# Transposing memory and seven token tiles by DMA instead of on TensorE in a two-layer decoder trunk

## The chip, the cores and the metric

The kernel runs on one core of one Trainium2 chip. The metric is the device time of one execution in microseconds (us). The kernel before takes 2338.09 us, the median of three runs (2337.59 to 2340.59).

## The reference, cut to what matters

The trunk has two layers. Each layer is a half-weighted SwiGLU block, a mixing block with three branches (stick-breaking attention, forgetting attention, attention to a memory), and a second half-weighted SwiGLU block, with an RMSNorm ahead of and behind each of them. There are 512 tokens of width 1024 and 256 memory rows of the same width, all float32.

```python
mem_n = _rmsnorm(mem, mem_norm_g)
for l in range(DEPTH):                                   # 2
    f = _swiglu(_rmsnorm(h, ffn1_pre_g[l]), ...)
    h = h + 0.5 * _rmsnorm(f, ffn1_post_g[l])

    u = _rmsnorm(h, mix_pre_g[l])
    proj = u @ w_in[l]
    ...
    k_mem, v_mem = jnp.split(mem_n @ w_mem_kv[l], 2, axis=-1)
    o_mem = _memory_attention(_split_heads(q_mem, ...), ...)
    ...
    h = h + _rmsnorm(merged @ w_out[l], mix_post_g[l])

    f = _swiglu(_rmsnorm(h, ffn2_pre_g[l]), ...)
    h = h + 0.5 * _rmsnorm(f, ffn2_post_g[l])
```

The normalised tokens `u` and the normalised memory `mem_n` are left factors of matrix products, so the kernel needs each of them with the features on the partitions: both must be transposed.

## The kernel before, in words

The 512 tokens are four tiles of 128 tokens by 1024 features (tile 0 to 3, `t`). To keep float32 accuracy on TensorE (PE), each operand is split into a high part `h` (a copy rounded by ScalarE, ACT) and a low part `l` (source minus high part, on VectorE, DVE); `mm3` issues three matmuls for each product, on source lines L212, L213 and L214. `split` makes the parts (L182 and L183, or L185 and L186 with a scale). So every weight block that arrives by DMA in a `raw_...` tile costs ACT a cast into `wh_...` of 128x1024 and DVE a subtraction into `wl_...`; only two `raw` buffers and four `wh` and four `wl` buffers exist for most of them, and SyncE (SP) issues all weight transfers from one queue in program order.

The place where one block ends and the next begins is called a border here. A class `Sub` handles it, with one object for each border: `a0` and `a1` stand between the first SwiGLU and mixing of layer 0 and layer 1, `b0` and `b1` between mixing and the second SwiGLU, `c0` between the two layers. At a border the last down projection (PSUM tiles `pda`, `pwo`, `pdc`) gives for each token tile:

- `result`: sums of squares (`sq...`, L544) and the scaled rows into a tile `fa`, `fb` or `fc`;
- `residual` (L575): the new token rows into `hfa`, `hm` or `hfc`, then their squares (L544 again);
- `normed` (L582): the normalised rows `u` back into `fa`, `fb`, `fc`, after a small chain of one-column steps (L486 to L500);
- `turned` (L592): eight PE transposes of 128x128 into two PSUM banks `uta`, `utb`, `utc`, and from there `split` with the scale into `us_a`, `us_b`, `us_c` (two ACT rows and two DVE rows of 128x512).

`chain` is the generator that does this for one tile, and `Q.weave` interleaves the chains with the queue of matrix products: a chain says ("wait", microseconds) for how much PE work is to be put in between. A scheduler then fixes one order of instructions for each engine when the program is built, and the engines run in that order, each waiting for what its next instruction needs.

At the borders `a0` and `a1` the memory is prepared too. `mem_norm` loads the two memory tiles `mraw` (128x1024), multiplies them by their reciprocal norms (L1063), transposes them with 16 PE transposes into PSUM tiles `mt` (L1070), and makes `mn` from these in eight ACT rows (L1075) and eight DVE rows (L1076) of 128x256, with the gain `memg`, which stands one feature to a partition. Then come the products for the memory's keys (`pmk`, weights `mk`) and values (`pmv`, weights `mv`), which need `mn` but no token; and then the first product that needs all four token tiles, the memory queries `pqm<-us_a,wh_qm`. Its job has the condition `src.ready(range(NT))`. At the borders `b` and `c` the first product (`pgc`, `pga`, L668) needs tiles 0 and 1.

Two 16-bit DMA transposes are already in the kernel before: in the token products (`turn`, L814, L815, L822, half planes of 128x1024 16-bit words) and in the stick-breaking heads (L1152, L1161, L1237).

The buffers that matter: the tag `rs` has one buffer of 128x1024 float32, and `v` has six.

Of the kernel before, what the change touches and what calls it, by code (L numbers as in the profile page):

```python
# [18 lines left out]
P = 128  # L19
# [4 lines left out]
def kernel(  # L24
# [57 lines left out]
    cst = ctx.enter_context(tc.tile_pool(name="cst", bufs=1))  # L82
# [6 lines left out]
    ident = cst.tile([P, P], F32, name="ident")  # L89
# [9 lines left out]
    def tmp(name):  # L99
        return sb.tile([P, S], F32, tag="f32t", bufs=8, name=name)  # L100
# [3 lines left out]
    def stile(shape, tag, name, dt=F32R):  # L104
        return sb.tile(shape, dt, tag=tag, bufs=BUFS[tag], name=name)
# [9 lines left out]
    memg = cst.tile([P, ND], F32, name="memg")  # L115
# [63 lines left out]
    def split(h_ap, l_ap, src, scale=None, later=False):  # L179

        if scale is None:
            both = [nc.scalar.copy(h_ap, src)]  # L182
            make = lambda: nc.vector.tensor_tensor(l_ap, src, h_ap.bitcast(F32), ALU.subtract)  # L183
# [173 lines left out]
    class Queue:  # L357
# [83 lines left out]
        def spawn(self, chain):  # L441
            self.chains.append([self.t, chain])
# [33 lines left out]
    HF = (slice(0, S), slice(S, D))  # L476
# [7 lines left out]
    RS = -16.0  # L484

    def rstd(st, a, b=None, beside=None):  # L486
# [13 lines left out]
        nc.vector.scalar_tensor_tensor(y, w, -3.0, y, ALU.add, ALU.mult)  # L500
        return y

    class Sub:

        def __init__(self, name, g_post, g_pre, half, tag, slack=0.0):

            self.slack = slack
# [93 lines left out]
    W_H, W_U = 4.8, (8.0, 7.0, 6.5, 4.5)  # L608


    NG = 2
# [5 lines left out]
    def ffn(l, src, wg, wu, wd, dst, name, spare, parked, plan, aside=None):  # L617
# [348 lines left out]
        if name == "a0":  # L966
            Q.add([], vectors)
# [69 lines left out]
    mem_rstd = cst.tile([P, MT, 2], F32, name="mem_rstd")  # L1037
# [10 lines left out]
    def mem_norm(l, mn):  # L1048

        mn[:] = [stile([P, ND, M], "tri", f"mn{l}_{i}") for i in range(2)]  # L1050
        raws = []
        if l == 0:
            ms, r = mem_rstd[:, :, 0], mem_rstd[:, :, 1]
            for out_, in_, f, s in ((r, ms, AF.Ln, 1.0), (r, r, AF.Exp, -0.5)):
                tc.keep_in_program_order(nc.scalar.activation(out_, in_, f, scale=s))
            nc.vector.tensor_tensor(ms, ms, r, ALU.mult)
            nc.vector.tensor_tensor(ms, ms, r, ALU.mult)
            nc.vector.tensor_scalar(ms, ms, -0.5, 1.5, ALU.mult, ALU.add)
            nc.vector.tensor_tensor(r, r, ms, ALU.mult)
        for t in range(MT):  # L1060
            raw = stile([P, D], "v", f"mraw{l}_{t}", F32)
            nc.sync.dma_start(raw[:], mem[0, t * P:(t + 1) * P, :])
            nc.vector.tensor_scalar(raw[:], raw[:], mem_rstd[:, t, 1:2], None, ALU.mult)  # L1063
            raws.append(raw)
        yield 0.0
        for i in range(ND // 2):
            pt = pbank("z", f"mt{l}_{i}")
            for j in range(2):
                for t in range(MT):
                    nc.tensor.transpose(pt[:, j * M + t * P:j * M + (t + 1) * P],  # L1070
                                        raws[t][:, (2 * i + j) * P:(2 * i + j + 1) * P], ident[:])
            for j in range(2):
                d = 2 * i + j
                src = pt[:, j * M:(j + 1) * M]
                nc.scalar.activation(mn[0][:, d], src, AF.Copy, scale=memg[:, d:d + 1])  # L1075
                nc.vector.scalar_tensor_tensor(mn[1][:, d], src, memg[:, d:d + 1],  # L1076
                                               mn[0][:, d].bitcast(F32), ALU.mult, ALU.subtract)
            yield 0.45

    def mem_kv(l, mn, ks, vs):  # L1080

# [539 lines left out]
    kvs = [([], []) for _ in LAYERS]  # L1621
    subs = [Sub("x", None, (0, 0), False, "k")]
    for l in LAYERS:
        subs.append(Sub(f"a{l}", (1, l), (2, l), True, "k", 4.0))
        subs.append(Sub(f"b{l}", (3, l), (4, l), False, "v"))
        subs.append(Sub(f"c{l}", (5, l), (0, l + 1) if l < L - 1 else None, True, "k"))

    def warm(n):

# [97 lines left out]
    for l in LAYERS:  # L1727
        i, mn = 3 * l, []
# [43 lines left out]
```

## Time and profile before

| | us |
|---|---|
| median of three runs | 2338.09 |
| lowest and highest run | 2337.59, 2340.59 |
| the profiled execution, its own time | 2342.67 |
| its span in the profile | 2340.9 |
| PE, PE's weight loads, DVE, ACT busy | 2322.9, 1960.2, 1764.2, 1509.8 |

The span runs from the first to the last recorded instruction; the profiled execution took 1.8 us more than its span and 4.6 us more than the median of the runs. A row of a timeline gives the start in us from the span's start, the length in us, the engine, the source line and what was written from what; in square brackets stands for how long the engine had been idle and what ended that. SPq is SyncE's queue of DMA issues.

### The profile page before, as it was taken

What the parts mean: (1) busy time and instruction counts of PE and PEld (TensorE: products, weight loads), DVE (VectorE), ACT (ScalarE), POOL (GpSimd) and SP (SyncE); (2) the same over time, 40 slices, a digit from 0 to 9 for tenths busy, and PEclk for the clock granted to TensorE, in tenths of its full rate; (3) what the DMA queues carried; (4) which work ended last, traced back from release to release, by engine and by line L of the source; (5) the groups of instructions that cost most, each with busy time, mean ns of one, the idle gap of its engine ahead of it and who ended that gap; (6) DMA issues with size and microseconds to landing.
All of it is one profiled execution on the core that took longest, in us unless ns stands there. A gap on an engine that the chain in (4) does not pass through costs nothing.

```text
span 2340.9 us, 30650 instructions
## 1 busy us (share of the span) xinstructions
PE 2322.9 (99%) x11463; PEld 1960.2 (84%) x11463; DVE 1764.2 (75%) x2253; ACT 1509.8 (64%) x2216; POOL 81.2 (3%) x182
## 2 busy tenths in 40 slices
PE   9999999999999999999999999999999999999998
PEld 7888888888888888888898888888888888888887
DVE  8877877566777688878798788765677767887785
ACT  6677465577756556775656774655787674667744
POOL 0000000000111000000000000000001100000000
PEclk9999999999999999999999999999999999999999
DMA  6667454344423555674646665544444236466744
GB/s 207 190 176 221 146 189 141 93 115 114 122 73 105 187 186 164 185 199 152 226 144 186 196 185 179 185 114 95 119 105 116 81 118 200 160 195 176 220 138 144
DMA packets 340344, 365.44 MB, mean 156 GB/s; under 512 B 120778, under 2 KB 231650, under 8 KB 340196
## 3 DMA queue, kind: packets, MB, share of 16 engines
q1 hardware_dynamic: 340100, 363.46, 52.0%
q8 instruction: 90, 1.47, 0.3%
q14 instruction: 58, 0.48, 0.1%
q0 software_dynamic: 96, 0.03, 0.0%
HBM read 319.39 MB, written 16.78 MB: 144 GB/s over the span
## 4 chain that ended last, share of the span: by engine, by line
PE 85%; DMA 5%; ACT 4%; DVE 3%; issue 2%; DVEq 0%; SPq 0%; ACTq 0%
PE pg L213 4%; PE pg L212 4%; PE pg L214 4%; PE pda L213 3%; PE pda L212 3%; PE pda L214 3%; PE pdc L213 3%; PE pdc L212 3%; PE pdc L214 3%; PE pb L213 1%; PE pb L212 1%; PE pb L214 1%; PE pq L213 1%; PE pq L212 1%; PE pq L214 1%
## 5 line engine op out<-in xcount | busy, mean ns | idle before, releaser
L212 PE MATMUL pg<-us_a,wh_wg 128*128 128x512 f32 x384 | 150.4, 392 | 0.0
L213 PE MATMUL pg<-us_a,wh_wg 128*128 128x512 f32 x384 | 149.7, 390 | 0.0
L214 PE MATMUL pg<-us_a,wl_wg 128*128 128x512 f32 x384 | 149.6, 390 | 0.0
L183 DVE TENSOR_TENSOR wl_da<-raw_da,wh_da 128x1024 fp32r<-128x1024 f32 x50 | 60.8, 1223 | 44.6 <-ACT wh_da L182 44.4
L183 DVE TENSOR_TENSOR wl_dc<-raw_dc,wh_dc 128x1024 fp32r<-128x1024 f32 x50 | 61.0, 1223 | 44.1 <-ACT wh_dc L182 44.1
L213 PE MATMUL pdc<-wl_dc,ahc 128*128 128x512 f32 x224 | 87.7, 392 | 0.0
L213 PE MATMUL pda<-wl_da,aha 128*128 128x512 f32 x224 | 87.6, 391 | 0.0
L214 PE MATMUL pdc<-wh_dc,alc 128*128 128x512 f32 x224 | 87.2, 389 | 0.0
L214 PE MATMUL pda<-wh_da,ala 128*128 128x512 f32 x224 | 87.2, 389 | 0.0
L212 PE MATMUL pdc<-wh_dc,ahc 128*128 128x512 f32 x224 | 86.6, 390 | 0.5 <-ACT pdc L895 0.5
L212 PE MATMUL pda<-wh_da,aha 128*128 128x512 f32 x224 | 86.5, 389 | 0.0
L186 DVE SCALAR_TENSOR_TENSOR wl_wg<-raw_wg,wh_wg 128x1024 fp32r<-128x1024 f32 x48 | 58.7, 1223 | 35.8 <-ACT wh_wg L185 35.6
L214 PEld LDWEIGHTS pg<-us_a,wl_wg 128*128 128x128 f32 x384 | 72.1, 188 | 15.1
L212 PEld LDWEIGHTS pg<-us_a,wh_wg 128*128 128x128 f32 x384 | 72.1, 188 | 14.2
L213 PEld LDWEIGHTS pg<-us_a,wh_wg 128*128 128x128 f32 x384 | 72.1, 188 | 14.2
L182 ACT CAST wh_da<-raw_da 128x1024 fp32r<-128x1024 f32 x50 | 52.1, 1050 | 46.9 <-PE pda L214 19.4
L182 ACT CAST wh_dc<-raw_dc 128x1024 fp32r<-128x1024 f32 x50 | 52.3, 1049 | 46.0 <-DMA raw_dc<-in_ffn_w_down_dram 13.9
L182 ACT CAST wh_uc<-raw_uc 128x1024 fp32r<-128x1024 f32 x44 | 46.4, 1054 | 34.5 <-PE pwc1g L214 7.7
L182 ACT CAST wh_ua<-raw_ua 128x1024 fp32r<-128x1024 f32 x44 | 46.2, 1052 | 30.2 <-PE pwa0g L214 7.6
L183 DVE TENSOR_TENSOR wl_uc<-raw_uc,wh_uc 128x1024 fp32r<-128x1024 f32 x44 | 53.7, 1220 | 14.5 <-ACT wh_uc L182 14.5
L183 DVE TENSOR_TENSOR wl_gc<-raw_gc,wh_gc 128x1024 fp32r<-128x1024 f32 x40 | 48.5, 1221 | 20.3 <-ACT wh_gc L182 20.3
L1237 ACT COPY pws<-ts 128x1024 uint16<-128x1024 uint16 (+1 forms) x64 | 55.4, 914 | 12.2 <-DMA ts<-ns 11.9
(643 smaller groups left out, 7921.1 us busy)
## 6 DMA issues: line engine op xcount, KB each, us to landing
raw_da<-in_ffn_w_down_dram SPq DMA_DIRECT2D x66, 512.0 KB, 5.3
raw_dc<-in_ffn_w_down_dram SPq DMA_DIRECT2D x66, 512.0 KB, 4.6
raw_ga<-in_ffn_w_gate_dram SPq DMA_DIRECT2D x52, 512.0 KB, 4.7
raw_ua<-in_ffn_w_up_dram SPq DMA_DIRECT2D x52, 512.0 KB, 4.5
raw_gc<-in_ffn_w_gate_dram SPq DMA_DIRECT2D x52, 512.0 KB, 4.1
raw_uc<-in_ffn_w_up_dram SPq DMA_DIRECT2D x52, 512.0 KB, 4.4
raw_wg<-in_w_gate_dram SPq DMA_DIRECT2D x48, 512.0 KB, 3.6
raw_wo<-in_w_out_dram SPq DMA_DIRECT2D x24, 512.0 KB, 3.7
```

The costliest lines, as they stand in the source:

```text
L182: both = [nc.scalar.copy(h_ap, src)]
L183: make = lambda: nc.vector.tensor_tensor(l_ap, src, h_ap.bitcast(F32), ALU.subtract)
L186: make = lambda: nc.vector.scalar_tensor_tensor(l_ap, src, scale, h_ap.bitcast(F32), ALU.mult, ALU.subtract)
L212: nc.tensor.matmul(pt, lh, rh, start=start, stop=False, skip_group_check=free)
L213: nc.tensor.matmul(pt, lh, rl, start=False, stop=False, skip_group_check=free)
L214: nc.tensor.matmul(pt, ll, rh, start=False, stop=stop, skip_group_check=free)
L1237: nc.scalar.copy(block_words(word, i), over[:, :, c:c + i + 1])
```

## The change

The 16 PE transposes of the memory in each layer and the eight PE transposes of some token tiles are replaced by a way through the DMA queue. `flip_out` copies the 128x1024 float32 words of a tile on ACT into two planes of 16-bit halves (128x2048 16-bit words) and issues one DMA transpose of the 128x2048 plane on SP's queue, back over the source tile; `flip_back` puts the two transposed halves together into words again, on ACT. The planes of a token tile stand in the one `rs` buffer, those of the memory in two `v` buffers. The high and low parts are then made from SBUF instead of PSUM. Which token tiles go this way is a new argument `flips`: tiles 0, 1 and 2 at the borders `a0` and `a1`, tile 0 at `b0`, `b1` and `c0` (nine tiles in all; `c1` ends the kernel and has no next block). Such a tile waits W_FLIP = 10.0 us of planned PE work between the two halves, where it had waited W_U[t] plus a slack of 4.0 at `a0` and `a1`.

The memory's gain is now a row, loaded by one more DMA per layer into `rs` (`grow`, `mg`) and multiplied in together with the reciprocal norm on DVE (two rows of 128x1024); the small transposed gain `memg`, its DMA, its transpose and its copy go away.

```diff
     def vectors():
...
-        nc.gpsimd.dma_start(vecs[0:ND, 0:P], mem_norm_g.rearrange("(d p) -> d p", p=P))
...
-        nc.tensor.transpose(pt[:, 0:ND], vecs[0:ND, 0:P], ident[0:ND, 0:ND])
...
-        nc.scalar.copy(memg[:], pt[:, 0:ND])
...
+    def flip_out(words, halves):
+        nc.scalar.copy(halves.bitcast(U16).rearrange("p (h k) -> p h k", h=2), words.bitcast(U16).rearrange("p (k h) -> p h k", h=2))
+        nc.sync.dma_start_transpose(words.bitcast(U16).rearrange("p (r q) -> p r q", q=P), halves.bitcast(U16))
+
+    def flip_back(words, over):
+        nc.scalar.copy(words.bitcast(U16).rearrange("p (k h) -> p h k", h=2), over.bitcast(U16).rearrange("p (h k) -> p h k", h=2))
...
                 self.normed(t)
+                if t in self.flips:
+                    halves = stile([P, D], "rs", f"fh{self.name}_{t}", F32)
+                    flip_out(self.fs[t][:], halves[:])
+                    yield ("wait", W_FLIP)
+                    flip_back(halves[:], self.fs[t][:])
+                    self.alloc()
+                    for hf in range(2):
+                        o = self.us[hf][:, :, :, t * P:(t + 1) * P]
+                        split(o[:, :, 0], o[:, :, 1], halves[:, HF[hf]].rearrange("p (e q) -> p e q", e=4), scale=RS)
+                    self.done.add(t)
+                    return
                 yield ("wait", W_U[t] + self.slack)
...
     def mem_norm(l, mn):
...
-        raws = []
+        raws, grow = [], stile([P, D], "rs", f"mg{l}", F32)
+        nc.sync.dma_start(grow[:], mem_norm_g.rearrange("(a d) -> a d", a=1).broadcast_to([P, D]))
...
-            nc.vector.tensor_scalar(raw[:], raw[:], mem_rstd[:, t, 1:2], None, ALU.mult)
+            nc.vector.scalar_tensor_tensor(raw[:], raw[:], mem_rstd[:, t, 1:2], grow[:], ALU.mult, ALU.mult)
...
-        for i in range(ND // 2):
-            pt = pbank("z", f"mt{l}_{i}")
...
+        for t, raw in enumerate(raws):
+            halves = stile([P, D], "v", f"mh{l}_{t}", F32)
+            flip_out(raw[:], halves[:])
...
+        for t, (raw, halves) in enumerate(zip(raws, turned)):
+            flip_back(halves[:], raw[:])
+            c = slice(t * P, (t + 1) * P)
+            split(mn[0][:, :, c], mn[1][:, :, c], halves[:].rearrange("p (d q) -> p d q", q=P))
...
+        subs.append(Sub(f"a{l}", (1, l), (2, l), True, "k", 4.0, (0, 1, 2)))
+        subs.append(Sub(f"b{l}", (3, l), (4, l), False, "v", flips=(0,)))
+        subs.append(Sub(f"c{l}", (5, l), (0, l + 1) if l < L - 1 else None, True, "k", flips=(0,)))
```

The change also moves instructions on the engines. In the rows below, the number behind a name's border and tile is the buffer's own; source lines of the kernel after are a few lower or higher (its cast is L178, its scaled copy L181, `flip_out` is L501 on ACT and L502 on SP, `flip_back` is L506).

**ACT at border `a0`, while tiles 0 and 1 are turned.** Before, the two scaled copies of each tile stand a few rows behind the casts of the memory's key weights:

```order
L182 CAST wh_mk_0_4_2772<-raw_mk_0_4_2648 128x1024
L182 CAST wh_mk_1_0_2934<-raw_mk_1_0_2770 128x1024
L544 ACTIVATE fa_2_1686,nha_2_2668<-hfa_2_2652 128x1024
L185 ACTIVATE us_a_0_2946<-uta_0_0_2948 128x4x128
L185 ACTIVATE us_a_1_2947<-uta_0_1_2955 128x4x128
L544 ACTIVATE sqa_3_0_2980,nfa_3_2665<-pda_0_3_2918 128x512
L185 ACTIVATE us_a_0_2946<-uta_1_0_3016 128x4x128
L185 ACTIVATE us_a_1_2947<-uta_1_1_3023 128x4x128
```

After, the flip of tile 0 stands in the same stretch, with the flip of tile 1 behind its last step:

```order
L501 COPY fha_0_2831<-fa_0_1683 128x2048
L178 CAST wh_mk_0_4_2746<-raw_mk_0_4_2644 128x1024
...
L506 COPY fha_0_2831<-fa_0_1683 128x2x1024
L549 ACTIVATE fa_2_1685,nha_2_2664<-hfa_2_2648 128x1024
L181 ACTIVATE us_a_0_2912<-fha_0_2831 128x4x128
L181 ACTIVATE us_a_1_2913<-fha_0_2831 128x4x128
L178 CAST wh_mk_1_4_2933<-raw_mk_1_4_2750 128x1024
L501 COPY fha_1_2858<-fa_1_1684 128x2048
L178 CAST wh_mv_0_2945<-raw_mv_0_2925 128x1024
```

Tile 1's copy out now stands behind tile 0's copies into `us_a`; tile 2's stands behind tile 1's in the same way, and the two flips of the memory stand ahead of all this, where its eight short rows were.

**SP at border `a0`.** Before, the queue holds weights and the parking of the token rows (`hsave`):

```order
L1549 DMA hsave<-hfa_1_2651 128x1024
L256 DMA raw_mk_1_0_2770<-in_w_mem_kv_dram 128x4x256
L1549 DMA hsave<-hfa_2_2652 128x1024
L256 DMA raw_mk_1_4_2776<-in_w_mem_kv_dram 128x4x256
L256 DMA raw_mv_0_2938<-in_w_mem_kv_dram 128x2x512
```

After, the transposes stand between them:

```order
L1564 DMA hsave<-hfa_1_2647 128x1024
L502 DMA_TRANSPOSE fa_0_1683<-fha_0_2831 128x16x128
L252 DMA raw_mk_1_4_2750<-in_w_mem_kv_dram 128x4x256
L252 DMA raw_mv_0_2925<-in_w_mem_kv_dram 128x2x512
L1564 DMA hsave<-hfa_2_2648 128x1024
L252 DMA raw_mv_2_2937<-in_w_mem_kv_dram 128x2x512
L502 DMA_TRANSPOSE fa_1_1684<-fha_1_2858 128x16x128
L252 DMA raw_mv_4_2949<-in_w_mem_kv_dram 128x2x512
```

The weight that stands behind a transpose is issued only after ACT has written that tile's planes.

**ACT at border `b0`, around the last weights of the down projection (`wo`).** Before:

```order
L182 CAST wh_wo_2_4_7349<-raw_wo_2_4_7341 128x1024
L185 ACTIVATE us_b_0_7487<-utb_0_0_7489 128x4x128
L185 ACTIVATE us_b_1_7488<-utb_0_1_7496 128x4x128
L544 ACTIVATE sqb_2_1_7509,nfb_2_7275<-pwo_1_2_7423 128x512
L544 ACTIVATE sqb_3_1_7512,nfb_3_7276<-pwo_1_3_7424 128x512
L182 CAST wh_wo_2_6_7355<-raw_wo_2_6_7347 128x1024
```

After:

```order
L501 COPY fhb_0_7398<-fb_0_7213 128x2048
L178 CAST wh_wo_2_2_7299<-raw_wo_2_2_7211 128x1024
...
L178 CAST wh_wo_2_4_7305<-raw_wo_2_4_7297 128x1024
L549 ACTIVATE sqb_2_1_7452,nfb_2_7231<-pwo_1_2_7379 128x512
L506 COPY fhb_0_7398<-fb_0_7213 128x2x1024
L178 CAST wh_wo_2_6_7311<-raw_wo_2_6_7303 128x1024
```

The cast of the last weight block now stands right behind the copy back, and `b1` has the same rows.

**ACT at border `c0`, ahead of the first product `pga`.** Before:

```order
L185 ACTIVATE us_c_0_10241<-utc_0_0_10243 128x4x128
L185 ACTIVATE us_c_1_10242<-utc_0_1_10250 128x4x128
L544 ACTIVATE sqc_2_0_10263,nfc_2_10037<-pdc_0_2_10227 128x512
L185 ACTIVATE us_c_0_10241<-utc_1_0_10286 128x4x128
...
L544 ACTIVATE fc_2_9076,nhc_2_10041<-hfc_2_10025 128x1024
```

After:

```order
L501 COPY fhc_0_10138<-fc_0_9024 128x2048
L549 ACTIVATE sqc_2_0_10200,nfc_2_9987<-pdc_0_2_10180 128x512
...
L181 ACTIVATE us_c_0_10224<-utc_1_0_10233 128x4x128
L549 ACTIVATE fc_2_9026,nhc_2_9991<-hfc_2_9975 128x1024
L506 COPY fhc_0_10138<-fc_0_9024 128x2x1024
L549 ACTIVATE sqc_3_0_10259,nfc_3_9988<-pdc_0_3_10210 128x512
L181 ACTIVATE us_c_0_10224<-fhc_0_10138 128x4x128
L181 ACTIVATE us_c_1_10225<-fhc_0_10138 128x4x128
```

Tile 0's scaled copies, which stood ahead of the squares of tile 2, stand behind them and behind the copy back.

More of the change, by code (lines that the diff above doesn't have):

```diff
@@ L113 @@
     gain_srcs = (ffn1_pre_g, ffn1_post_g, mix_pre_g, mix_post_g, ffn2_pre_g, ffn2_post_g)
-    memg = cst.tile([P, ND], F32, name="memg")
     nbgate = cst.tile([P, L, 3 * ND], F32, name="nbgate")
@@ L501, in rstd, with __init__ @@
         return y
+    def flip_out(words, halves):
[3 more added lines that the diff above has]
+        nc.scalar.copy(words.bitcast(U16).rearrange("p (k h) -> p h k", h=2), over.bitcast(U16).rearrange("p (h k) -> p h k", h=2))
     class Sub:
-        def __init__(self, name, g_post, g_pre, half, tag, slack=0.0):
-            self.slack = slack
+        def __init__(self, name, g_post, g_pre, half, tag, slack=0.0, flips=()):
+            self.slack, self.flips = slack, flips
             self.name, self.g_post, self.g_pre, self.half, self.tag = name, g_post, g_pre, half, tag
@@ L605, in chain @@
                 yield ("pe", 0.9)
-    W_H, W_U = 4.8, (8.0, 7.0, 6.5, 4.5)
+    W_H, W_U, W_FLIP = 4.8, (8.0, 7.0, 6.5, 4.5), 10.0
     NG = 2
@@ L1062, in mem_norm @@
             nc.sync.dma_start(raw[:], mem[0, t * P:(t + 1) * P, :])
-            nc.vector.tensor_scalar(raw[:], raw[:], mem_rstd[:, t, 1:2], None, ALU.mult)
+            nc.vector.scalar_tensor_tensor(raw[:], raw[:], mem_rstd[:, t, 1:2], grow[:], ALU.mult, ALU.mult)
             raws.append(raw)
         yield 0.0
-        for i in range(ND // 2):
-            pt = pbank("z", f"mt{l}_{i}")
[L1068 to L1078, printed above, removed]
+        turned = []
+        for t, raw in enumerate(raws):
+            halves = stile([P, D], "v", f"mh{l}_{t}", F32)
+            flip_out(raw[:], halves[:])
+            turned.append(halves)
+            yield 0.0
+        for t, (raw, halves) in enumerate(zip(raws, turned)):
+            flip_back(halves[:], raw[:])
+            c = slice(t * P, (t + 1) * P)
+            split(mn[0][:, :, c], mn[1][:, :, c], halves[:].rearrange("p (d q) -> p d q", q=P))
+            yield 0.0
     def mem_kv(l, mn, ks, vs):
```

3 lines of the change are left out of this document (removed).

## Prediction

> **What bounds the kernel now.** I read the page first: busy shares and the chain that ended last.
>
> ```profile
> PE 2322.9 (99%) x11463; PEld 1960.2 (84%) x11463; DVE 1764.2 (75%) x2253; ACT 1509.8 (64%) x2216; POOL 81.2 (3%) x182
> PE 85%; DMA 5%; ACT 4%; DVE 3%; issue 2%; DVEq 0%; SPq 0%; ACTq 0%
> ```
>
> PE is never long without work, so a PE instruction less is worth its place in PE's row of starts, as long as PE still finds its operands. The waits of PE, longest first, say how little it waits (first, fifth and last row of eleven; the longest single wait among them is 1.2):
>
> ```profile
> PE pwo L213 <- DVE wl_wo L183: 2.6, 4, 0.9
> PE mt L1070 <- DVE mraw L1063: 1.2, 3, 0.5
> ...
> PE pga L668 <- ACT w_ga L182: 0.2, 1, 0.2
> ```
>
> The question is then whether the stretches in which the change adds work to ACT have room there. The view of stretches gives ACT's busy time (fourth group) from the first sum of squares at `a0` and `a1` to the first memory-query product:
>
> ```profile
> core 0: us, PE busy (x) PEld busy (x) DVE busy (x) ACT busy (x) POOL busy (x), PEclk, DMA share, GB/s
> 322.64:373.71 51.07, 50.53 (x293) 44.00 (x292) 44.25 (x80) 35.06 (x79) 0.00 (x0) 1.00 0.44 145
> 1484.13:1534.64 50.51, 50.14 (x288) 43.72 (x288) 42.08 (x73) 32.91 (x74) 0.00 (x0) 1.00 0.42 136
> ```
>
> ACT is free for 16.0 and 17.6 us of these stretches, much less than its 36% over the whole span would suggest, and DVE is fuller still (44.3 and 42.1).
>
> **The gain: 105 PE transposes.** The timeline of PE at `a0` shows eight transposes of a token tile and the memory's sixteen, with their neighbours:
>
> ```profile
> 345.94 0.39 PE L213 MATMUL pda<-wl_da,hida 128*128 128x512 f32 x1
> 346.17 0.39 PE L214 MATMUL pda<-wh_da,hida 128*128 128x512 f32 x1
> 346.40 1.03 PE L592 MATMUL uta<-ident,fa 128*128 128x128 f32 x8
> 347.19 0.48 PE L212 MATMUL pda<-wh_da,hida 128*128 128x512 f32 x1
> 347.50 0.40 PE L213 MATMUL pda<-wl_da,hida 128*128 128x512 f32 x1
> ...
> 325.97 0.39 PE L212 MATMUL pda<-wh_da,hida 128*128 128x512 f32 x1
> 326.88 2.19 PE L1070 MATMUL mt<-ident,mraw 128*128 128x128 f32 x16 [0.53 <-DVE mraw L1063]
> 328.83 0.48 PE L213 MATMUL pda<-wl_da,hida 128*128 128x512 f32 x1
> 329.14 0.40 PE L214 MATMUL pda<-wh_da,hida 128*128 128x512 f32 x1
> ```
>
> Matmuls of 128x512 start 0.23 apart (346.17 less 345.94). From 346.17 to 347.50 are 1.33, two steps would be 0.46: a token tile's transposes cost 0.87. From 325.97 to 329.14 are 3.17, less 0.46: the memory costs 2.7, its waits included. Nine tiles and two memories are 7.8 + 5.4 = 13.2 us; the lone gain transpose adds some 0.15. Full gain: 13.4 us, if nothing waits in its place. At `a0` and at `a1` it is 2.7 + 3 x 0.87 = 5.3 each.
>
> **The cost on ACT.** Half-size copies of the same two kinds are in the token products, with the DMA transpose between them:
>
> ```profile
> L814 ACT COPY tha0u<-sa x16: 1037/1042/1065, 94.1 to 202.6; 128x1024 uint16<-128x1024 uint16 x16
> L822 ACT COPY hra<-tra0u x16: 1349/1360/1370, 98.4 to 215.9; 128x1024 uint16<-128x1024 uint16 x16
> L815 SPq DMA_TRANSPOSE trc0u<-thc0u x16: 1231/1232/2807, 923.9 to 1035.5; - x16
> DMA to landing us min/median/max: 3.0/3.5/8.1
> L1075 ACT ACTIVATE mn<-mt,memg x16: 465/482/509, 328.1 to 1491.4; 128x256 fp32r<-128x256 f32 x16
> L182 ACT CAST wh_da<-raw_da 128x1024 fp32r<-128x1024 f32 x50 | 52.1, 1050 | 46.9 <-PE pda L214 19.4
> ```
>
> The new copies are twice as wide: 2 x 1.04 = 2.1 out, 2 x 1.36 = 2.7 back, 4.8 for a flip. The scaled copies into `us` stay. At `a0` and `a1` ACT gets five flips (24.0) and two casts of 1.05 for `mn`, and loses eight rows of 0.48: 24.0 + 2.1 - 3.9 = 22.2 us more. ACT would be busy 35.1 + 22.2 = 57.3 and 32.9 + 22.2 = 55.1 us before the queries can start, in stretches of 51.1 and 50.5. Without one idle moment the queries start at 322.64 + 57.3 = 379.9 and 1484.13 + 55.1 = 1539.2. Before:
>
> ```profile
> 373.71 0.39 PE L212 MATMUL pqm<-us_a,wh_qm 128*128 128x512 f32 x1
> 1534.64 0.39 PE L212 MATMUL pqm<-us_a,wh_qm 128*128 128x512 f32 x1
> ```
>
> So the floor is a loss of 6.2 and 4.6 us, PE's gain there already used up: its own work could have been done at 368.4, and it waits. Nothing else stands in its order before the queries that could fill the gap.
>
> **The ring at `a0` and `a1`.** ACT will not be without idle time, because the three tiles pass one `rs` buffer one after another. One round is copy out 2.1, DMA, copy back 2.7, two scaled copies (1.1), DVE's two low parts before the buffer is free (about 0.6 of them uncovered), and one or two other ACT rows of 1.05 that stand between copy back and the next copy out. For the DMA of twice the bytes I take 5.0: the half takes 3.5 at the median, twice that would be 7.0, and plain transfers of the same 512 KB land in 3.7 to 5.3:
>
> ```profile
> raw_wo<-in_w_out_dram SPq DMA_DIRECT2D x24, 512.0 KB, 3.7
> raw_da<-in_ffn_w_down_dram SPq DMA_DIRECT2D x66, 512.0 KB, 5.3
> ```
>
> 5.0 is nearest to the latter, which run at the same borders beside other weights; the ends are 3.5 and 8.1. Round: 2.1 + 5.0 + 2.7 + 1.1 + 0.6 + 1.0 = 12.5. [...]
>
> When does the first round start? Before, tile 0 was squared and normalised here:
>
> ```profile
> 332.95 1.06 ACT L544 ACTIVATE fa<-hfa 128x1024 f32<-128x1024 f32 x1 [0.27 <-DVE hfa L575]
> 339.37 1.28 DVE L582 SCALAR_TENSOR_TENSOR fa<-hfa,nha,gqa 128x1024 f32<-128x1024 f32 x1
> ```
>
> After, ACT's order has both memory flips (9.6), both `mn` casts (2.1) and a weight cast (1.1) ahead of that square, less the eight short rows (3.9) and with some 1.5 of waiting for the landing: the square moves from 333.0 to about 343.4. Some of that was idle on the rest of tile 0's way, and I get its normalised row ready at 348.9 instead of 340.7. Three rounds: 348.9 + 37.5 = 386.4, against 373.71: a loss of 12.7 at `a0`. Summing ACT's rows from 1484.13 in the same way I get the first copy out at `a1` at 1506.4 and three rounds at 1543.9; two more casts (`wh_mv`) than at `a0` stand inside the rounds, so 1545: a loss of 10.4. PE's waits spread: on the `mn` parts, since six `pmk` products now stand ahead of the last tile's down projection; on that projection's PSUM preload (a copy behind the flips on ACT); on `wl_mk` and `wl_mv`, late because ACT's casts are, and because SP issues the next weights behind a transpose that waits for ACT; then on `us_a`. DVE gives up eight short rows and two scalings and gets four of 128x1024, about even, hidden under ACT's wait. SP gets 13 issues of 1.23 and two gain rows, on a queue that mostly waits for buffers; the gain rows stand some forty rows ahead of their use, and POOL loses one small DMA: nothing for these.
>
> **Borders `b0` and `b1`.** PE was already waiting there for the last `wo` block:
>
> ```profile
> 822.98 1.28 DVE L582 SCALAR_TENSOR_TENSOR fb<-hm,nhb,gqb 128x1024 f32<-128x1024 f32 x1
> 833.36 1.05 ACT L182 CAST wh_wo<-raw_wo 128x1024 fp32r<-128x1024 f32 x1 [0.99 <-DMA raw_wo<-in_w_out_dram]
> 834.44 1.23 DVE L183 TENSOR_TENSOR wl_wo<-raw_wo,wh_wo 128x1024 fp32r<-128x1024 f32 x1 [0.56 <-ACT wh_wo L182]
> 835.72 0.50 PE L213 MATMUL pwo<-wl_wo,ms 128*128 128x512 f32 x1 [0.75 <-DVE wl_wo L183]
> ```
>
> After, that cast stands behind the copy back: normalised 824.3, out 826.4, landed 831.5, back 834.2 at the earliest, cast 835.2, low part 836.4, against 835.7. The transpose shares the DMA engines with `raw_wo`, so I take +1.0 at each, 2.0 in all, and the 0.87 saved there is swallowed by the wait. Ends: -0.9 (all on time) and +3.
>
> **Border `c0`.** Here the tile is normalised late and the next product soon needs it:
>
> ```profile
> 1167.46 1.27 DVE L582 SCALAR_TENSOR_TENSOR fc<-hfc,nhc,gqc 128x1024 f32<-128x1024 f32 x1
> 1175.76 1.06 ACT L544 ACTIVATE fc<-hfc 128x1024 f32<-128x1024 f32 x1 [2.27 <-DVE hfc L575]
> 1175.87 0.64 PE L668 MATMUL pga<-us_c,w_ga 128*128 128x256 f32 x4
> ```
>
> Normalised at 1168.7, out 1170.8, landed 1175.9; the copy back stands behind the squares of tile 2, so it starts at 1176.8 and ends at 1179.5; then one sum of squares (0.6) and a scaled copy (0.5): 1180.6 against 1175.87, a loss of 4.7. Ends: 0 and +8.
>
> **Sum.** 12.7 + 10.4 + 2.0 + 4.7 = 29.8, less the 0.15 of the gain's transpose: 29.6 us. Against the profiled execution's own time that is 2342.67 + 29.6 = 2372.3; against the median of the runs, 4.6 lower, 2338.1 + 29.6 = 2367.7, which is my time. PE's transposes are counted in the start times that I compare, so their gain is in it.
>
> **Rivals.** A change under 0.2% (4.7 us) is about what a measurement of this kernel cannot tell from none.
>
> *The flips are hidden.* If PE never waits at `a0`, `a1`, `c0`, the whole 13.4 us are gained: 2338.1 - 13.4 = 2324.7. For it: PE has 20 us of memory products to run in between. Against it: ACT's sum alone passes the stretch. It decides if the 128x2048 copies cost half of what I take, 12 us less in each stretch, as nothing in these rows suggests. Chance 0.10; about even, within 4.7 us, 0.05.
>
> *Only ACT's queue binds.* If the landing takes 3.5 and the ring hides behind ACT's other rows, only the floor is lost: 6.2 + 4.6, `b` -0.9 twice, `c0` +2: 2338.1 + 11 = 2349. Chance 0.15.
>
> *PE loses speed by waiting.* At the start, after nothing to do, eight transposes took 2.03 us, against 1.03 in the row at 346.40:
>
> ```profile
> 8.46 2.03 PE L1661 MATMUL utx<-ident,fx 128*128 128x128 f32 x8
> 14.61 0.62 PE L668 MATMUL pga<-us_x,w_ga 128*128 128x256 f32 x3 [0.21 <-ACT w_ga L182]
> ```
>
> If a wait of several us brings that state back, half of the following time is lost, at most 6.7 us (half of the 13.4 from the first matmul at 1.2 to 14.6). Waits that long I expect once or twice at each of `a0`, `a1` and once at `c0`; at half of that price for three, +10: 2378. No wait of PE before is longer than 1.2 us, so no row shows the point where it begins. [...] Chance 0.14.
>
> *My sum,* at 2367.7, has the rest, 0.56. The ends of the DMA, 3.5 and 8.1 in place of 5.0, move six rounds by -9 and +19, `c0` by less. Range 2345 to 2390: it takes in the floor, the slower clock and both ends of the DMA, and leaves out the gain and no change. Faster 0.10, same 0.05, slower 0.85.
>
> **What the profile after would show.** Right: `pqm` starts 10 us or more later at both layers; PE's waits name `us_a`, `mn` and `wl_mk` or `wl_mv`; ACT is busy over 90% in the two stretches; copies take 2.1 and 2.7. Wrong, if copies of 128x2048 are no longer than those of 128x1024, if the landing is under 4 us, or if PE's waits stay near the sum of before.

## The result: 38.6 us slower

The changed kernel takes 2377.4 us, the median of five runs (2374.51 to 2380.34), against 2338.91 for the kernel before on the same chip (2337.59 to 2341.13). The ratio is 1.0165, with a 95% interval of 1.0151 to 1.0179. Below, "x us slower" is always a ratio less one, times 2338; 0.1% of it is 2.3 us. Nine token tiles take the new way (three at each of `a0` and `a1`, one at each of `b0`, `b1` and `c0`); the seven of the title is a miscount. One run of an experiment below, with the tokens of `a0` and `a1` only, took 10844.02 us, and its ratio goes by its other four.

The profiled execution took 2376.4 us, with a span of 2374.6. Engine shares and chain of the changed kernel:

```profile
PE 2325.7 (98%) x11358; PEld 1956.6 (82%) x11358; DVE 1763.5 (74%) x2241; ACT 1559.1 (66%) x2229; POOL 78.9 (3%) x181
PE 80%; DMA 7%; ACT 6%; DVE 4%; issue 2%; SPq 0%; ACTq 0%; DVEq 0%
```

PE has 105 instructions less and is busy 2.8 us longer; ACT is busy 49.3 us more. DMA and ACT gain at PE's cost in the chain. PE's waits (total us, times, longest) show where:

```profile
PE pqm L208 <- ACT us_a L181: 16.2, 2, 9.9
PE pmk L208 <- DVE nha L496: 4.7, 1, 4.7
PE pga L684 <- ACT us_c L181: 4.2, 1, 4.2
PE pwo L208 <- ACT wh_wo L178: 3.0, 2, 1.8
...
PE pda L208 <- ACT pda L860: 2.2, 1, 2.2
```

Before, the longest single wait was 1.2; now the first memory query waits 16.2 us in its two layers. PE's timeline shows when these products start (in brackets the wait ahead of them); before, they started at 373.71, 1175.87 and 1534.64:

```profile
385.83 1.22 PE L208 MATMUL pqm<-us_a,wh_qm 128*128 128x512 f32 x2 [6.29 <-ACT us_a L181]
1192.88 1.74 PE L684 MATMUL pga<-us_c,w_ga 128*128 128x256 f32 x8 [4.23 <-ACT us_c L181]
1565.32 1.22 PE L208 MATMUL pqm<-us_a,wh_qm 128*128 128x512 f32 x2 [9.91 <-ACT us_a L181]
```

The lag is 12.1 us at `a0`, 17.0 at `c0`, 30.7 at `a1` and 33.7 at the end of the spans. It is 38.6 between the runs, because the profiled execution shown of before is some 4 us above the median of its runs; where that matters, a second reference is used below.

The rows of ACT at `a0` that belong to the token flips show the ring of one `rs` buffer (L501 copies out, L506 copies back, L181 is the scaled copy that releases PE):

```profile
347.31 1.90 ACT L501 COPY fha<-fa 128x2048 uint16<-128x2048 uint16 x1 [0.50 <-DVE fa L587]
...
355.23 2.55 ACT L506 COPY fha<-fa 128x2048 uint16<-128x2048 uint16 x1
...
360.66 1.90 ACT L501 COPY fha<-fa 128x2048 uint16<-128x2048 uint16 x1
...
367.99 2.50 ACT L506 COPY fha<-fa 128x2048 uint16<-128x2048 uint16 x1
...
374.43 1.89 ACT L501 COPY fha<-fa 128x2048 uint16<-128x2048 uint16 x1
...
381.88 2.47 ACT L506 COPY fha<-fa 128x2048 uint16<-128x2048 uint16 x1 [0.59 <-DMA fa<-fha]
...
385.16 1.15 ACT L181 ACTIVATE us_a<-fha 128x512 fp32r<-128x512 f32 x2
```

No tile goes out before the one ahead of it is finished. The rounds are 13.3 and 13.8 us, the last 11.4 up to PE's start.

### The profile page after: what moved, and what is told of

Its sections match the earlier page's. It is cut to its first block, busy times and chain, and to the rows that moved or that the text cites. A ratio compares the mean times of both kernels' runs of the same rounds, so it can differ in the third digit from the quotient of the medians.

```text
span 2374.6 us, 30461 instructions
## 1 busy us (share of the span) xinstructions
PE 2325.7 (98%) x11358; PEld 1956.6 (82%) x11358; DVE 1763.5 (74%) x2241; ACT 1559.1 (66%) x2229; POOL 78.9 (3%) x181
## 4 chain that ended last, share of the span: by engine, by line
PE 80%; DMA 7%; ACT 6%; DVE 4%; issue 2%; SPq 0%; ACTq 0%; DVEq 0%
PE pg L209 4%; PE pg L208 4%; PE pg L210 4%; PE pdc L209 2%; PE pdc L208 2%; PE pdc L210 2%; PE pda L209 2%; PE pda L208 2%; PE pda L210 2%; PE pb L208 1%; PE pb L209 1%; PE pb L210 1%; PE pq L208 1%; PE pq L209 1%; PE pq L210 1%
## 5 line engine op out<-in xcount | busy, mean ns | idle before, releaser
L178 ACT CAST wh_dc<-raw_dc 128x1024 fp32r<-128x1024 f32 x50 | 52.2, 1049 | 48.0 <-PE pdc L210 16.4
L178 ACT CAST wh_da<-raw_da 128x1024 fp32r<-128x1024 f32 x50 | 52.0, 1048 | 45.9 <-PE pda L210 16.2
L178 ACT CAST wh_uc<-raw_uc 128x1024 fp32r<-128x1024 f32 x44 | 46.3, 1053 | 32.6 <-PE pwc1g L210 8.6
L178 ACT CAST wh_ua<-raw_ua 128x1024 fp32r<-128x1024 f32 x44 | 46.2, 1053 | 30.0 <-PE pwa0g L210 7.8
L179 DVE TENSOR_TENSOR wl_ua<-raw_ua,wh_ua 128x1024 fp32r<-128x1024 f32 x44 | 53.6, 1220 | 13.9 <-ACT wh_ua L178 13.8
L179 DVE TENSOR_TENSOR wl_ga<-raw_ga,wh_ga 128x1024 fp32r<-128x1024 f32 x40 | 48.5, 1220 | 19.7 <-ACT wh_ga L178 19.7
L181 ACT ACTIVATE wh_wg<-raw_wg 128x1024 fp32r<-128x1024 f32 x48 | 50.9, 1060 | 17.9 <-PE pv L1140 10.5
```

## The experiments

Each kernel was timed beside the kernel before on the same chip; the time given is the median of its runs.

### Each part alone

Memory only: tokens back on PE.

```diff
-        subs.append(Sub(f"a{l}", (1, l), (2, l), True, "k", 4.0, (0, 1, 2)))
-        subs.append(Sub(f"b{l}", (3, l), (4, l), False, "v", flips=(0,)))
-        subs.append(Sub(f"c{l}", (5, l), (0, l + 1) if l < L - 1 else None, True, "k", flips=(0,)))
+        subs.append(Sub(f"a{l}", (1, l), (2, l), True, "k", 4.0, ()))
+        subs.append(Sub(f"b{l}", (3, l), (4, l), False, "v", flips=()))
+        subs.append(Sub(f"c{l}", (5, l), (0, l + 1) if l < L - 1 else None, True, "k", flips=()))
```

> Only the memory goes through the DMA, all token tiles are transposed on TensorE again. ACT then has 2 flips of 4.4 us (1.9 out and 2.5 back, as measured in the changed kernel) and two casts of 1.05 in place of eight rows of 0.48 in each layer: 7.0 us more in stretches where it had 16.0 and 17.6 idle. My theory (the loss is the one-buffer ring of token tiles behind a full ACT queue) expects the 2.7 us of the memory's transposes to be gained in each layer, less at most a short wait for mn: -5 us, between -6 and 0, and mn ready at about 345.5 us with the first pmk at about 346. The rival that the memory's flips are a main part of the loss (they hold up ACT's sums of squares and casts) expects +5 us or more and a wait of PE over 2 us at the first pmk.

Measured: 2343.85 us, ratio 1.0024 (1.0015 to 1.0033), 5.6 us slower. My expectation failed; the rival held. The wait is at the first `pmk`. Rows of PE, ACT and DVE of this kernel ahead of it:

```profile
345.48 0.55 PE L208 MATMUL pmk<-mn,wh_mk 128*128 128x256 f32 x1 [4.52 <-DVE nha L496]
```
```profile
337.15 2.51 ACT L506 COPY mh<-mraw 128x2048 uint16<-128x2048 uint16 x1
...
342.56 0.57 ACT L549 ACTIVATE sqa<-pda 128x512 f32<-128x512 f32 x1
...
343.97 0.58 ACT L549 ACTIVATE sqa<-pda 128x512 f32<-128x512 f32 x1
```
```profile
344.65 0.68 DVE L554 SCALAR_TENSOR_TENSOR fa<-pda,gpa 128x512 f32<-128x512 f32 x1
```

PE had finished the down projection at about 341. Its three sums of squares on ACT stand behind the second copy back and its casts, and DVE's scaled rows (L554), which read the same PSUM tiles, behind other rows in turn. PE resumes 0.15 us after the first of these rows ends (344.65 + 0.68 = 345.33). I read this as the PSUM bank coming free late, with `mn` itself done by 343; the profile names only the DVE row that ended last. So ACT's total over a stretch, put at 42.1 of 51 us here, was not the test: the copies stand in one lump ahead of rows that PE needs.

Tokens of `a0` and `a1` only: memory as before, `flips=()` at `b` and `c`.

> Only tiles 0, 1 and 2 at the borders a0 and a1 go through the DMA; memory and the tiles at b and c are on TensorE as before. ACT gets 3 x 4.4 = 13.2 us more: 48.3 and 46.1 us in stretches of 51.1 and 50.5, so it would just fit. My theory (one rs buffer, rounds of 13 us one after the other, as measured 13.3 to 13.8 in the changed kernel) expects the first copy out at about 341 and 1500 (in the clock of the kernel before), three rounds after it pqm at about 380 and 1539, 6.5 and 4.1 us later than before, and a wait of PE of 7 to 9 us just ahead of each, followed by a few us at half clock: +11 us without and +16 with the clock. The rival that only ACT's queue binds expects no loss here: -5 us, and no wait of PE for us_a over 2 us.

Measured: 2354.44 us, ratio 1.0066 (1.0053 to 1.0080), 15.4 us slower. The first copy out and the first query:

```profile
338.59 1.90 ACT L505 COPY fha<-fa 128x2048 uint16<-128x2048 uint16 x1
```
```profile
377.58 1.65 PE L212 MATMUL pqm<-us_a,wh_qm 128*128 128x512 f32 x3 [5.60 <-ACT us_a L185]
```

Three rounds in 39.0 us, as expected: the ring holds PE where ACT has room. By ACT's sum alone (48.3 us put, in a stretch of 51.1) nothing would have been lost here. The time fits the +16 with the clock (granted 0.96 over 320 to 400, some 3 us missing), but the waits did not have the size expected: 5.6 and 3.2 us, not 7 to 9. In the changed kernel, with the memory's flips ahead of it on ACT, the same ring begins 8.7 us later (347.31).

Memory, and one tile at `a0` and `a1` (`(0,)` there, none at `b` and `c`).

> Memory and only tile 0 at a0 and a1 go through the DMA; tiles 1 and 2 there, and those at b and c, are on TensorE. One round of the ring is left, and ACT has 11.4 us more to do, under its idle time of 16.0 and 17.6. My theory expects no wait for us_a and PE's gain of 2.7 + 0.87 a layer, less short waits for mn: -5 us, between -7 and 0. If the loss belonged to each flip in equal parts (33.7 us in the two profiles, less about 7 at b and c, over ten flips at a: 2.7 each), six flips would give +16.

Measured: 2347.79 us, ratio 1.0044 (1.0031 to 1.0056), 10.3 us slower. Neither number came. Without the ring, PE never waits for `us_a`, but the wait of 4.6 for `pmk` stays, and one more flip in each layer adds 4.7 us to the memory's 5.6, although it saves 2 x 0.87 of transposes.

Borders `b` and `c` only.

> Only tile 0 at b0, b1 and c0 goes through the DMA; borders a and the memory as before. In the changed kernel PE fell back 0.5 us at b0, 4.3 at c0 and 2.4 at b1 by its starts. My theory (each border loses by its own copies) expects about +7 us, most of it at c0, with a wait of PE for us_c of about 4 us and half clock behind it. The rival that these slips are left over from the border a (later weights, another phase of the queues) expects PE's gain of 3 x 0.87: -2.6 us.

Measured: 2347.28 us, ratio 1.0043 (1.0031 to 1.0056), 10.1 us slower. The slips are these borders' own, and larger than the 7 us expected. Two waits of PE:

```profile
PE pga L688 <- ACT us_c L185: 3.8, 1, 3.8
PE pwo L212 <- ACT wh_wo L182: 3.7, 2, 2.7
```

The three parts alone make 5.6 + 15.4 + 10.1 = 31.1; together they make 38.6.

### What in a flip costs: the way taken apart

No copies and no DMA transpose; the parts are made from the untransposed tiles.

```diff
     def flip_out(words, halves):
-        nc.scalar.copy(halves..., words...)
-        nc.sync.dma_start_transpose(words..., halves...)
+        pass
     def flip_back(words, over):
-        nc.scalar.copy(words..., over...)
+        pass
```

> The changed kernel without the way through the DMA: no copies on ACT, no DMA transposes; the high and low parts are made straight from the untransposed tiles, so nothing that these tiles feed is transposed. All other rows stay. This measures the gain by itself: the prediction put it at 13.4 us for 105 transposes, so 2324.7, if nothing waits in their place. The rival that TensorE's transposes were partly free (it waited for weights beside them) expects 2330 or more.

Measured: 2327.01 us, ratio 0.9953 (0.9940 to 0.9965): 11.0 us faster, between 8.2 and 14.0. The predicted gain of 13.4 lies in the interval.

Copies without the transpose.

```diff
     def flip_out(words, halves):
         nc.scalar.copy(halves..., words...)
-        nc.sync.dma_start_transpose(words..., halves...)
```

> The changed kernel with both ACT copies of each flip but without the DMA transpose between them: the copy back reads the source tile again, so nothing is transposed. A round of the ring loses its landing of 5.2 us: 13 becomes about 8. My theory (copies on ACT, then the ring) expects that ACT's queue alone then sets pqm (about 380 and 1539 in the clock of the kernel before, 6.2 and 4.6 late), that PE still waits about 4.5 us at the first pmk, and about 1 us at c0: 2345 to 2352. The rival that landing and ring make nearly the whole loss expects 2325 to 2335.

Measured: 2350.38 us, ratio 1.0058 (1.0046 to 1.0071), 13.6 us slower. Its time is as expected, and `pqm` starts at 379.38, near the 379.9 that ACT's sum had given. That agreement is partly luck: PE itself came there only 0.2 us earlier. Its waits stand elsewhere, and the expected ones at the first `pmk` and at `c0` are not among them:

```profile
PE pda L208 <- ACT pda L859: 11.8, 2, 6.4
```

PE now waits for ACT to preload the PSUM tiles of the down projection, a copy of 128x512 that takes 0.59 us, behind the memory's of 2.5 us. The copies cost 11.0 + 13.6 = 24.6 us by themselves.

A plain DMA without the copies.

```diff
     def flip_out(words, halves):
-        nc.scalar.copy(halves..., words...)
-        nc.sync.dma_start_transpose(words..., halves...)
+        nc.sync.dma_start(halves, words)
     def flip_back(words, over):
-        nc.scalar.copy(words..., over...)
+        pass
```

> The changed kernel without the two ACT copies of each flip; a plain DMA copy of the same 512 KB from the tile to its buffer stands in place of the transpose, so nothing is transposed. A round is the landing of about 5, scaled copies and low parts 1.7 and some waiting, 8 to 9 us: three rounds from 341 end at 365 to 368, before PE's own work is done. My theory expects no wait for us_a over 2 us, no wait of 4.5 us at the first pmk, and 2326 to 2335. The rival that it is the landing that holds (ring, and rows queued behind it) expects 2345 or more.

Measured: 2327.22 us, ratio 0.9952 (0.9938 to 0.9966), 11.2 us faster: the same as with no way at all.

```profile
368.41 0.39 PE L208 MATMUL pqm<-us_a,wh_qm 128*128 128x512 f32 x1
```

PE starts the query without a wait, at the 368.4 that the prediction had put for its own work (to the tenth by chance: the executions of one kernel differ by some us). The test changes the kind of transfer too: these plain copies land in 2.9 to 4.6 us, the transposes in 4.5 to 5.6, and a plain copy holds SyncE's queue for 0.5 us, a transpose for 1.5 to 3.6. No run gives the price of either alone. With that reserve, 512 KB through the queue and the single buffer cost nothing here without ACT in the round (2327.22 against 2327.01); with the two copies the same step costs the remaining 25.0 (38.6 - 13.6).

### The ring

```diff
-                    halves = stile([P, D], "rs", f"fh{self.name}_{t}", F32)
+                    halves = stile([P, D], "v" if t == 1 else "rs", f"fh{self.name}_{t}", F32)
```

> The changed kernel, but the halves of tile 1 at a0 and a1 stand in a buffer of the tag v instead of the one rs buffer, so tiles 0 and 1 are on their way at once. The copies, casts and transfers are the same in number. In the changed kernel the three rounds took 13.3, 13.8 and 11.9 us from 347.3 on. My theory (the ring of one buffer) expects about one round less between the first copy out and pqm, until ACT's queue alone binds (pqm at about 380 at a0; 5 to 6 us earlier at each of a0 and a1): 11 us less than the changed kernel's 2377, so about 2366, and a wait of PE for us_a of 1 to 4 us at each. The rival that ACT's queue alone sets the end expects the same time as with one buffer, 2377, within 2 us.

Measured: 2366.2 us, ratio 1.0126 (1.0112 to 1.0139), against 1.0165 with one buffer: some 9 to 11 us less, as expected, with not one copy or transfer less. The remaining wait moved:

```profile
PE pmv L208 <- DVE mk L179: 8.2, 1, 8.2
PE pmv L208 <- DVE nha L487: 7.0, 1, 7.0
```

PE does not wait for `us_a` any more, but 7 and 8 us earlier, at the memory's values. In ACT's new order two flips stand ahead of the copies of `pmk` out of PSUM. I had expected 1 to 4 us at `us_a`; the place was wrong.

### The copies on GpSimd

```diff
-        nc.scalar.copy(
+        nc.gpsimd.tensor_copy(
```

in `flip_out` and `flip_back`, once for all 13 flips and once for the memory alone.

> The changed kernel with the copies out and back of all 13 flips on GpSimd, which does nothing in these stretches. A copy of 64x1024 words takes 1.04 us there in the kernel before, so I estimate 2.1 to 4 us for 128x2048 halves. ACT loses 22 us of copies in each layer's stretch at a. My theory (ACT's queue and the one buffer together) expects the casts and sums of squares in time and the rounds still serial: 2.1 to 4 + 5.2 + 2.1 to 4 + 1.1 + 0.6, that is 11 to 15 us a round: at 11 pqm about 4 us earlier than in the changed kernel at each layer and a total of about 2362; at 15 no better than 2377. The rival that ACT's queue alone binds expects PE's 13 us back: about 2330 to 2340 whatever the copies take.

> Only the memory goes through the DMA, with its copies on GpSimd; compared with the same on ACT, which was 5.8 us slower than the kernel before. There PE waited 4.5 us at the first pmk while ACT's sums of squares of the down projection stood behind the copies, so that its PSUM bank came free late. That theory expects the wait of 4.5 to go, and the 2.7 us a layer to be gained: about 2333 to 2336, if a copy on GpSimd takes under 3 us; with longer ones mn itself is late and the wait stays. The rival (mn's way through the DMA is too long for its place, whoever copies) expects 2344 as with the copies on ACT.

Measured: 2375.27 us (1.0162, 1.0148 to 1.0175) for all, 2343.01 us (1.0022, 1.0013 to 1.0032) for the memory alone. Neither differs from the same on ACT, so an idle engine was no way out. For all 13 flips the rounds at `a0` stayed at 14.4 and 13.3 us, near the slow end of what was expected. For the memory the 2333 to 2336 of my theory did not come: the wait at the first `pmk` went, but others took its place. GpSimd and two groups of DVE's one-column rows in the memory's kernel (min, median, max in ns; the kernel before has 0.21 and 0.16 us for such rows):

```profile
L506 POOL COPY mh<-mraw x4: 2502/2978/3491, 332.5 to 1498.3; 128x2048 uint16<-128x2048 uint16 x4
```
```profile
L495 DVE SCALAR_TENSOR_TENSOR nfa<-nfa x2: 1126/1772/2417, 326.8 to 335.9; 128x1 f32<-128x1 f32 x2
L496 DVE SCALAR_TENSOR_TENSOR nfa<-nfa x2: 148/972/1795, 328.0 to 338.4; 128x1 f32<-128x1 f32 x2
```

While GpSimd copies (325.2 to 329.7 and 332.5 to 338.4), a DVE row of one column takes up to 2.4 us, and the copies take up to 3.5 in place of 2.5. DVE's queue became what ACT's had been, as the largest of PE's waits in this kernel shows:

```profile
PE pda L209 <- DVE wl_da L179: 6.5, 4, 3.8
```

### The slow clock

> The changed kernel with 22 (layer 0) and 38 (layer 1) extra matmuls of 128x512 on a tile of zeros, written to the PSUM tile of the first memory query and then overwritten, just ahead of that query: 5.0 and 8.6 us of work for TensorE inside the waits of 6.45 and 10.07 us for us_a. They add no work for another engine. The theory that the waits cost a second time by the clock (granted 0.5 for 6.8 and 10.2 us behind these two waits; PE fell back a further 2.9 and 2.0 us there by its starts) expects the granted clock to stay at 1.0 behind pqm and about 5 us less than the changed kernel: 2372. The rival that the slow clock there is free (other waits would take its place) expects 2377, and the extra matmuls to cost nothing.

Measured: 2376.95 us, ratio 1.0169 (1.0155 to 1.0183): no change. The test does not settle it, because the clock fell with the fill too: waits of 3.0 us were left ahead of `pqm`, and the granted clock behind them was 0.87 and 0.79. From the first query to the next product in the filled kernel (PE's busy time is the second number, its granted clock the third from the end):

```profile
387.32:400.60 13.28, 12.68 (x49) 10.09 (x49) 5.60 (x8) 3.61 (x7) 1.40 (x3) 0.87 0.29 80
1566.47:1580.86 14.39, 13.86 (x48) 10.85 (x49) 3.79 (x5) 2.13 (x4) 1.18 (x3) 0.79 0.14 36
```

The missing clock is 13.28 x 0.13 + 14.39 x 0.21 = 4.7 us, against 13.80 x 0.19 + 12.90 x 0.13 = 4.3 in the changed kernel, where a part of the missing clock passed inside the waits (granted 0.88 over 379.54 to 385.83 and 0.66 over 1555.41 to 1565.32). The queries also start 1.49 and 1.15 us later, because the last copy back waits 2.1 and 2.2 us for its landing, against 0.6 and 0.5. What the trace of the changed kernel shows is this; the same stretch, before (first two rows) and after:

```profile
373.71:384.59 10.88, 10.88 (x50) 9.01 (x49) 6.16 (x9) 4.99 (x8) 0.00 (x0) 1.00 0.56 147
1534.64:1545.52 10.88, 10.88 (x49) 9.01 (x48) 6.87 (x9) 5.94 (x9) 0.00 (x0) 1.00 0.57 157
```
```profile
385.83:399.63 13.80, 13.68 (x48) 10.60 (x49) 5.60 (x8) 3.61 (x7) 1.40 (x3) 0.81 0.30 78
1565.32:1578.22 12.90, 12.90 (x49) 10.35 (x50) 3.79 (x5) 2.13 (x4) 1.18 (x3) 0.87 0.16 42
```

The same work takes 2.9 and 2.0 us longer, without a wait; the missing clock is 2.6 and 1.7 of that.

### A version that beats both

The costs above are those of copies at a full border, not of missing transposes. So the last kernel takes away only what layer 1 repeats: it stores the memory's transposed parts at layer 0 and loads them at layer 1.

```diff
+    mkeep = nc.dram_tensor("mkeep", (2, P, ND, M), F32, kind="Internal").ap()
     def mem_norm(l, mn):
         mn[:] = [...]
+        if l:
+            for i in range(2):
+                nc.sync.dma_start(mn[i][:].bitcast(F32), mkeep[i])
+            yield 0.0
+            return
...
+        for i in range(2):
+            nc.gpsimd.dma_start(mkeep[i], mn[i][:].bitcast(F32))
```

> The kernel before, not the changed one, with the memory's transposed high and low parts written to DRAM at layer 0 and loaded from there at layer 1, where its 16 transposes and the 16 rows of ACT and DVE behind them go away: two loads of 1 MB in place of two of 512 KB. It takes TensorE's work away without a copy on ACT at the border. If the 2.7 us of a memory's transposes are worth their place, it takes 2335.4 against 2338.1. If the larger loads come late or hold up SyncE's queue, PE waits at layer 1's first pmk and it takes 2338 or more.

Measured: 2335.66 us, ratio 0.9989 (0.9980 to 0.9998): 2.6 us faster, where 2.7 had been expected. That is smaller than the 0.2% used as a bound here, but the interval excludes no change. Eight rows each of ACT and DVE behind the transposes go away too, so the gain need not be the transposes' alone.

## Why the prediction was right, and where its sizes were off

**The sign and the mechanism.** Slower was forecast, from ACT's copies and the ring of one buffer at `a0` and `a1`, and both are shown: copies without a landing lose 13.6, a plain transfer without copies loses nothing, and a second buffer takes 9 to 11 off. The wait that was put on `mn` came as 4.7 us at the first `pmk`, but it named `nha`, not `mn`, whose last part was done at 343.0, 2.5 us before PE went on.

**The gain.** 13.4 was put, 11.0 measured (8.2 to 14.0).

**The copies and the landing.** Estimated 2.1 and 2.7, and 5.0. The rows of the changed kernel (the third line belongs to the DMA transposes):

```profile
L501 ACT COPY fha<-fa x6: 1888/1897/1899, 347.3 to 1554.2; 128x2048 uint16<-128x2048 uint16 x6
L506 ACT COPY fha<-fa x6: 2466/2523/2572, 355.2 to 1561.4; 128x2048 uint16<-128x2048 uint16 x6
DMA to landing us min/median/max: 4.5/5.2/5.6
```

1.9 and 2.5, and 5.2. In the kernel with a plain DMA, copies of the same tiles at the same places landed in 3.1 at the median, so the choice of 5.0, and not of the 3.7 of `wo`, was right. The 13 issues, put at 1.23 us and at nothing in the sum, held SyncE's queue for 1.5 to 3.6 us each; no run gives their price by itself.

**`a0` and `a1`.** The first copy out was put at 348.9, three rounds of 12.5 behind it, `pqm` at 386.4. It came at 347.31, 38.5 us of rounds, 385.83. At `a1` 10.4 was put; between `pga` and the second `pqm` the lag grew by 13.7, of which 1.7 are the half clock behind `pga` (below). ACT's busy share was put over 90%; it was 86% and 88%:

```profile
322.34:385.83 63.49, 50.16 (x252) 41.18 (x250) 44.50 (x74) 54.88 (x85) 0.00 (x0) 0.93 0.61 166
1502.33:1565.32 62.99, 49.30 (x253) 40.49 (x251) 44.21 (x72) 55.19 (x85) 0.00 (x0) 0.92 0.69 177
```

**`b0` and `c0`.** 5.7 was put for both. Against the profiled execution of before, the lag grew by 4.9 between the first query and `pga`; 2.9 of that is the longer stretch behind `pqm`, and 2.0 is left. The last kernel above is the kernel before up to `a1`, apart from two stores at `a0`, with a profiled execution 2.2 us below its own median; its first query and its first product after `c0`:

```profile
372.19 0.39 PE L212 MATMUL pqm<-us_a,wh_qm 128*128 128x512 f32 x1
1172.41 2.08 PE L668 MATMUL pga<-us_c,w_ga 128*128 128x256 f32 x16
```

Against these the changed kernel is 13.6 and 20.5 late, 6.8 more, which leaves 3.9. So 2 to 4 us were lost at `b0` and `c0`. In the kernel with the borders `b` and `c` alone (first query at 373.00, `pga` at 1179.67) the same two references give 4.5 and 6.5, on both sides of the 5.7; why these borders lose less in the changed kernel stays open.

**What was left out of the sum.** The time was forecast at 2367.7, 9.7 short. The rival in which PE loses speed by waiting was priced at +10 but kept apart, though the waits behind which it was expected were the sum's own. It came as well. Four stretches of the changed kernel behind which no wait on the ring takes the loss up again:

```profile
386.00:392.00 6.00, 5.89 (x15) 4.17 (x16) 3.51 (x6) 1.77 (x4) 1.40 (x3) 0.57 0.65 169
1192.00:1197.00 5.00, 4.12 (x22) 4.13 (x23) 4.66 (x11) 2.71 (x10) 0.00 (x0) 0.66 1.04 402
1565.00:1570.00 5.00, 4.68 (x13) 3.59 (x14) 2.19 (x3) 0.78 (x2) 1.18 (x3) 0.62 0.40 107
2029.00:2033.00 4.00, 4.00 (x12) 3.12 (x11) 4.00 (x8) 2.89 (x6) 0.00 (x0) 0.57 0.49 131
```

The missing clock in them is worth 6 x 0.43 + 5 x 0.34 + 5 x 0.38 + 4 x 0.43 = 7.9 us. 29.6 + 7.9 = 37.5, against 38.6 measured. That so little is left is partly luck: `b0` and `c0` were put too high and `a1` too low, and the two errors partly cancel. The same holds for the rival's own 2378, which took three equal prices of 3.35. The share of the clock is worked out from the trace; the filled kernel, in which as much of the clock is missing, neither confirms nor denies it. The rival had also read the slow rows at the start of the kernel as this state; the granted clock there, over 1.20 to 14.60, is 1.00, so those rows do not show it. The rows behind the waits do: over 386 to 388 the granted clock is 0.50.

**The rivals that fell.** "Hidden" named its own condition, cheaper copies, and the kernel without copies meets it (2327.22 against 2324.7 put). "Only ACT's queue binds" put 2349; without the landing 2350.38 remain, though with PE's waits at the PSUM preloads and not at `us_a`.

**In the experiments,** what failed was to judge the memory's flips, and one token flip, by ACT's total over the stretch. Each delayed short rows that PE needed at once.

## What to carry to other kernels

Moving work off the busiest engine paid here only where the helper's rows fitted between the rows that the busy engine waits for (11.2 us faster without ACT's copies, 13.6 slower with them and without the landing): look at what stands behind each new long row in the helper's order (PSUM preloads, sums of squares, casts), not at the busy share. A way through a single buffer cost the whole round (copy, landing, copy back, use; 13.3 and 13.8 us) for each tile; either half of the round alone may fit (ahead of `pqm` at `a0` PE waited 0.23 us without the landing, and not at all without the copies). When a forecast contains waits of several us on TensorE, put the slower clock behind them into the sum (here 0.57 to 0.66 was granted over four stretches, an estimate of 7.9 of 38.6 us).

## What the runs showed that was not expected

A wait of 2.18 us at the same place (`pda`, at `a1`) was followed by full clock in the kernel with the memory alone, and by a lower one in the kernel with one tile more. PE's row after the wait, and the stretch behind it, of the one and of the other:

```profile
1506.50 0.50 PE L208 MATMUL pda<-wh_da,hida 128*128 128x512 f32 x1 [2.18 <-ACT pda L860]
```
```profile
1506.00:1512.00 6.00, 5.50 (x30) 4.69 (x31) 5.92 (x12) 4.87 (x10) 0.00 (x0) 1.00 0.52 181
```
```profile
1509.49 0.51 PE L208 MATMUL pda<-wh_da,hida 128*128 128x512 f32 x1 [2.18 <-ACT pda L860]
```
```profile
1510.00:1515.00 5.00, 5.00 (x16) 3.92 (x16) 4.75 (x6) 3.73 (x4) 0.00 (x0) 0.66 0.50 184
```

Other waits just ahead do not explain it: one of 0.30 stood there in the first kernel and one of 0.76 in the second, but in the changed kernel, with one of 0.29, the same wait of 2.18 (at 1523.65) was followed by 0.57 over 1524 to 1528.

How long the slow clock lasted can be estimated from the missing clock: 0.50 was granted over 386 to 388 and over 1566 to 1568, so the time at half clock is twice what is missing. That gives 3.4 us over 1187 to 1200 at 0.87, 6.9 over 379.40 to 399.63 at 0.83, and 10.2 over 1554.00 to 1578.22 at 0.79, close to one, two and three times 3.4. Why a wait of 2.18 us was followed by it in two kernels and not in a third is not shown.

DVE's one-column rows of up to 2.4 us beside GpSimd's copies were not expected either, and no run shows what holds them up. Not every row was slow there: one with a single tensor input (L489, 326.10) beside the first of these copies took 0.21 us, as in the kernel before.
